# Attention with grouped keys: values cast to DRAM by batch and filled over SyncE, GpSimd transfers placed in planned gaps

## The chip, the cores and the metric

The kernel runs on one core of a Trainium2 chip. The metric is the device time of one execution in microseconds (us). It is measured in several runs, of which the median is taken. One more execution is recorded by the hardware profiler, and all rows of instructions below come from it.

## The reference

Grouped-query attention: 8 batches, 8 query heads, 2 heads of keys and values (each serves 4 query heads), 1024 positions, head size 64, all in float32.

```
scores = scale * np.matmul(q_group, k_group.transpose(0, 1, 3, 2))
scores_max = np.max(scores, axis=-1, keepdims=True)
attn = np.exp(scores - scores_max)
attn = attn / (np.sum(attn, axis=-1, keepdims=True) + 1e-08)
output[:, q_start:q_end, :, :] = np.matmul(attn, v_group)
```

The inputs are small (0.1 times a normal draw), and the kernel takes the exponential without subtracting the maximum.

## The kernel before, in words

**Tiling.** One query head of one batch is a job; there are 64 jobs. A job has 8 chunks of 128 keys. For a chunk, two matmuls (L856) write the scores of 128 keys against 1024 queries into one of three PSUM slots `sp`: keys lie on the partitions. The exponential of 372 of the 512 chunks is taken by ScalarE (L866, tile `pt`). That of the other 140 is made by VectorE from bits: a pass over PSUM writes 16-bit integers `yt` (L877); two operations on bits take from them a mantissa `zt` (L884) and a power of two `et` (L891), for two chunks at a time (2048 columns); and a multiplication `zt = yt * zt` (L900) corrects the mantissa. Part of the columns of this multiplication is given to GpSimd (L829), 107 times in all. These are called products below. TensorE then multiplies 128 x 128 blocks of `pt`, `et` and `zt` with the values `va`, which carry a column of ones, so that the sums of the softmax come along (L918). VectorE takes the reciprocal (L983), scales into `ost` (L992), and SyncE stores (L996).

**Order.** A class `Plan` lays out the work of ScalarE, VectorE and TensorE ahead of time with fixed costs (the `M_` constants, in ns) and gives a list of events with due times. The kernel emits instructions in the order of these times, and each engine runs its own list in that order. The order of scores, exponentials, passes and products is therefore fixed when the kernel is built. A product on GpSimd is made to wait for the instruction of VectorE that stands before it, so that it starts as VectorE begins a pass over PSUM.

**Transfers.** Queries and keys are first cast from float32 to bfloat16 by a transfer that GpSimd issues from DRAM to DRAM (`cast_q`, `cast_k`, both through `cast`, L617; the tiles `qd`, `kd`). One transfer of queries takes two heads, one of keys takes both heads of a batch. SyncE then brings them into SBUF transposed: `turn_q` (L677) and `turn_k` (L667), whose result is doubled with the two halves exchanged by `copy_k` (L671, L672). Values are cast straight into SBUF: for each of the 15 groups (a batch and one of its two heads of keys and values) after the first, `cast_v` (L659) issues two transfers from GpSimd into one of four buffers `va`. The values of the first group come another way and are not touched.

The due times of these transfers hang on `at`, the planned time of a job's first score: 19 us ahead for keys, 18 for queries, 12 for values. Once the first product has been emitted, a cast that becomes due is put into a list and begun behind a product if the planned gap to the next product is longer than `M_ISSUE`, 650 ns:

```
nth += 1
while casts and starts[nth] > free + M_ISSUE:
    begin(*casts.pop(0)[1:], False)
    free += M_ISSUE
```

A cast that is over 5 us overdue is begun at once. Each engine's instructions run in order, so a product behind a cast on GpSimd waits for the cast's issue, and on SyncE a copy of `kt` or a store waits for all that stand before it.

Of the kernel before, what the change touches and what calls it, by code (L numbers as in the profile page):

```python
# [10 lines left out]
M_START = 5450  # L11
# [25 lines left out]
M_GLEAD = 160  # L37
M_GFIX = 190
M_GCOL = 1.88
# [2 lines left out]
M_NORM = 531  # L42
M_HOLD = 1500
M_SPARE = 800
M_ISSUE = 650

M_GAP = 90
M_RUNWAY = 2100
# [9 lines left out]
INF = float("inf")  # L58
# [479 lines left out]
def kernel(  # L538
# [7 lines left out]
    nc = tc.nc  # L546
    FP32 = mybir.dt.float32
    BF16 = mybir.dt.bfloat16
# [5 lines left out]
    B, H, S, D = q.shape  # L554
    G = k.shape[1]
# [3 lines left out]
    HS = S // 2  # L559
# [10 lines left out]
    NVA = 4  # L570
    plan = Plan(NJ, NPT - 2, NCT - 1, NYT - 2)

    dram = ctx.enter_context(tc.tile_pool(name="dram", bufs=1, space=bass.MemoryType.DRAM))
# [34 lines left out]
    va = [kvp.tile([128, NH, 2, D + 1], BF16, name=f"va{i}") for i in range(NVA)]  # L608
# [2 lines left out]
    nc.vector.memset(warm, 0.0)  # L611
    for t in va:
        nc.vector.memset(t[:, :, :, D : D + 1], 1.0)
    kt, qt, qd, kd, vs = {}, {}, {}, {}, {}

    def cast(src, t):
        return nc.gpsimd.dma_start(  # L617
            out=t.rearrange("(a x) d -> a (x d)", a=128),
            in_=src.rearrange("(a x) d -> a (x d)", a=128),
        )  # L620

    def cast_q(j):
        b, h = divmod(j, H)
        if j == NJ - 1:
            t = qd[j] = dram.tile([HS, 2 * D], BF16, name=f"qd{j}")
            return nc.gpsimd.dma_start(  # L626
                out=t.rearrange("(c p) d -> p c d", p=128), in_=rows(q[b, h], True)
            )
        n = 2 if 3 < j < NJ - 2 else 1
        t = dram.tile([n * HS, 2 * D], BF16, name=f"qd{j}")  # L630
        for i in range(n):
            qd[j + i] = t[i * HS : (i + 1) * HS, :]
        return cast(q.rearrange("b h s d -> (b h s) d")[j * S : (j + n) * S, :], t)
# [9 lines left out]
    def rows(x, fours=False):  # L643
        how = "(p c two) d -> p c (two d)" if fours else "(c p two) d -> p c (two d)"
        return x.rearrange(how, p=128, two=2)
# [9 lines left out]
            in_=vs.pop((b, g)).rearrange("p c (two d) -> p c two d", two=2),  # L655
        )

    def cast_v(b, g, two):
        return nc.gpsimd.dma_start(  # L659
            out=va[(b * G + g) % NVA][:, :, two, 0:D],  # L660
            in_=v[b, g].rearrange("(c p two) d -> p c two d", p=128, two=2)[:, :, two, :],
        )

    def turn_k(b, g):
        t = ktp.tile([128, 2, HS], BF16, name="kt")
        kt[(b, g)] = t
        nc.sync.dma_start_transpose(out=t[:, 0:1, :], in_=kd[(b, g)])  # L667

    def copy_k(b, g):
        t = kt[(b, g)]  # L670
        nc.sync.dma_start(out=t[D : 2 * D, 1, :], in_=t[0:D, 0, :])  # L671
        nc.sync.dma_start(out=t[0:D, 1, :], in_=t[D : 2 * D, 0, :])  # L672
# [69 lines left out]
    for c in range(NH):  # L742
        for half in range(2):
            lo = half * D
# [12 lines left out]
    ev = list(plan.ev)  # L757
    n = len(ev)
    for j in range(NJ):
        b, h = divmod(j, H)  # L760
        at = need[j]
        g = h // HPG
        if h % HPG == 0 and j:
            if g == 0 or b == 0:
                ev.append((max(at - 19000, M_START + 200), "ck", None, (b, g), None))
            ev.append((at - 12500, "tk", None, (b, g), None))
            ev.append((at - 4000, "cp", None, (b, g), None))
            for two in range(2):
                ev.append((at - 12000, "cv", None, (b, g, two), None))
        if j == 0:  # L770
            ev.append((M_START + 100, "pl", None, (b, g), None))
        if j == 3 or (j > 3 and j % 2 == 0) or j == NJ - 1:
            ev.append((max(at - 18000, M_START + 100), "cq", None, j, None))
        if j > 1:
            ev.append((max(at - 11000, M_START + 100 * j), "tq", None, j, None))
    for x in [e for e in plan.ev if e[1] == "norm"]:
        lo, hi = x[2]
# [13 lines left out]
    def flat(t):  # L791
        return t.bitcast(BF16).rearrange("p i a b -> p (i a b)")
# [11 lines left out]
                yield ci, pt[(j, c)][:, par, :]  # L804

    begun = [e for e in ev if e[1] == "gmul"]
    starts = [e[0] + M_GLEAD for e in begun] + [INF]
    nth, free = 0, 0
    casts = []
    vec, gps = None, None  # L810

    def begin(kind, j, gate):
        ins = cast_q(j) if kind == "cq" else (cast_k if kind == "ck" else cast_v)(*j)
        if now and gate:
            tc.add_manual_dep(ins.ins, now.ins.name, Sync, reason="loads in time, not sooner")

    for when, kind, x, j, c, *cols in ev:
        if casts and casts[0][0] < when - 5000:
            begin(*casts.pop(0)[1:], True)
        if kind in ("ck", "cq", "cv"):  # L820

            if gps is None:
                begin(kind, j, True)
            else:
                casts.append((when, kind, j))
        elif kind == "gmul":
            lo, w = c
            z = flat(zt[j])[:, lo : lo + w]
            gps = nc.gpsimd.tensor_tensor(  # L829
                out=z, in0=flat(yt[j])[:, lo : lo + w], in1=z, op=ALU.mult  # L830
            )
            tc.add_manual_dep(gps.ins, vec.ins.name, Sync, reason="VectorE needs the port before")

            took = M_GFIX + M_GCOL * w
            free = max(free, when + M_GLEAD) + took
            nth += 1
            while casts and starts[nth] > free + M_ISSUE:
                begin(*casts.pop(0)[1:], False)
                free += M_ISSUE
        elif kind == "tk":  # L840
            turn_k(*j)
        elif kind == "cp":
            copy_k(*j)
        elif kind == "tq":
# [3 lines left out]
        elif kind == "score":  # L848
            b, h = divmod(j, H)
            t = kt[(b, h // HPG)]  # L850
            where_s[(j, c)] = new_slot(x)

            for half in range(2):
                lo = half * D
# [8 lines left out]
        elif kind == "act":  # L863
            p = pp.tile([128, 2, HS], BF16, name="pt")
# [7 lines left out]
        elif kind == "dpass":  # L872
            ch, i = j
            where[c] = j
            if i == 0:
                yt[ch] = yp.tile([128, CHN, 2, HS], U16, name="yt")
            vec = nc.vector.tensor_scalar(  # L877
                out=yt[ch][:, i, :, :], in0=where_s[c],
                scalar1=EXP_A, scalar2=EXP_B, op0=ALU.mult, op1=ALU.add,
            )  # L880
        elif kind == "zh":
# [3 lines left out]
                out=zt[j][:, 0:c], in0=yt[j][:, 0:c], scalar1=0x7F, scalar2=0x3F00,  # L885
                op0=ALU.bitwise_and, op1=ALU.bitwise_or,
            )
        elif kind == "two":
# [3 lines left out]
                out=et[j][:, 0:c], in0=yt[j][:, 0:c], scalar1=0x7F80, scalar2=None,  # L892
# [5 lines left out]
        elif kind == "mul":  # L898
            z = flat(zt[j])[:, 0 : cols[0]]
            vec = nc.vector.tensor_tensor(  # L900
                out=z, in0=flat(yt[j])[:, 0 : cols[0]], in1=z, op=ALU.mult
            )
        elif kind == "add":
            z = zt[j].bitcast(BF16)[:, 0:c]
            vec = nc.vector.tensor_tensor(
                out=z, in0=et[j].bitcast(BF16)[:, 0:c], in1=z, op=ALU.add
            )
        elif kind == "pv":
            job, piece = divmod(x, NPIECE)
            b, h = divmod(job, H)  # L910
            qs, par = divmod(piece, 2)
            lo = (x - plan.groups[plan.group_of[x]][0]) * (D + 1)
# [3 lines left out]
            for i in range(j, j + c):  # L916
                ci, p = every[i]
# [9 lines left out]
        elif kind == "pvf":  # L927
# [4 lines left out]
            for i in range(NPIECE):  # L932
# [3 lines left out]
                lo = i % 4 * (D + 1)  # L936
# [9 lines left out]
        elif kind == "pvl":  # L946
            b, h = divmod(NJ - 1, H)
# [3 lines left out]
            for i in range(NPIECE):  # L951
# [4 lines left out]
                lo = i % 4 * (D + 1)  # L956
# [9 lines left out]
        elif kind in ("rec", "norm"):  # L966
            lo, hi = x
            n = hi - lo
# [24 lines left out]
        elif kind == "store":  # L993
            b, h = divmod(j, H)
            r = place_of(j * NPIECE)
            ins = nc.sync.dma_start(  # L996
                out=rows(out[b, h], j in (0, NJ - 1)),
                in_=ost[:, r : r + NPIECE, :].rearrange("p (s two) d -> p s (two d)", two=2),
# [32 lines left out]
```

## Time and profile before

| what | value |
|---|---|
| time, median of 3 runs | 360.22 us (359.57 to 360.33) |
| the profiled execution, its own time | 360.52 us |
| its span, first to last instruction | 358.7 us |
| granted clock of TensorE | 1.00 |
| mean busy share of the DMA engines from 100 to 200 us | 0.76 |
| GpSimd: casts of values, of queries and keys | 30 of 858 ns, 41 of about 615 ns |
| GpSimd: products | 107 of 1240 ns |

Rows of the profile name the line of the kernel, the engine (PE is TensorE, PEld its weight loads, DVE VectorE, ACT ScalarE, POOL GpSimd, SP SyncE), the operation, what is written and read, and how often. After the bar stand the busy time in us and the mean length of one in ns; after the second bar the idle time of the engine ahead of such instructions, and what ended it. In a timeline the first number is the start in us, the second the length in us of what is merged in the row, and the bracket gives idle time before it. In a list of waits a row has who waited, for whom, the sum in us, the number and the longest. A q after an engine's name means its instruction queue.

### The profile page before, as it was taken

How to read it: one execution, taken by the hardware profiler on the slowest of the kernel's cores; microseconds unless marked ns; L12 is line 12 of the kernel's file. 1: busy time of each engine (PE TensorE's matmuls, PEld its weight loads, DVE VectorE, ACT ScalarE, POOL GpSimd, SP SyncE). 2: the span in 40 equal slices, each digit the busy share in tenths (PEclk: the TensorE clock that was granted, in tenths of full speed). 3: DMA queues.
4: the chain of work that ended last, by engine and by line, in shares of the span. 5: the costliest groups of instructions: out<-in, count | busy, mean ns of one | idle time of the engine just before them, and what ended most of it. 6: DMA issues, size and time to landing. Idle time of an engine off the chain costs nothing.

```text
span 358.7 us, 14051 instructions
## 1 busy us (share of the span) xinstructions
PE 346.6 (97%) x6236; PEld 222.4 (62%) x6236; DVE 348.4 (97%) x516; ACT 346.3 (97%) x376; POOL 182.9 (51%) x186
## 2 busy tenths in 40 slices
PE   8899999999999999999999999999999999999994
PEld 3556666666666666666566666566666666666664
DVE  4999999999999999999999999999999999999994
ACT  5999999999999999999999999999999999999991
POOL 4227656575375645566485755455655626670000
PEclk9999999999999999999999999999999999999999
DMA  6955959279686954888567786837969687594233
GB/s 146 134 103 106 162 116 134 50 127 142 133 135 119 149 134 76 129 137 123 121 87 136 148 134 112 134 103 114 107 135 120 133 151 103 120 114 109 37 101 106
DMA packets 96173, 42.87 MB, mean 119 GB/s; under 512 B 61024, under 2 KB 94944, under 8 KB 95456
## 3 DMA queue, kind: packets, MB, share of 16 engines
q1 hardware_dynamic: 78288, 29.51, 39.0%
q0 software_dynamic: 17680, 12.19, 31.3%
q8 instruction: 49, 0.80, 1.0%
q10 hardware_dynamic: 144, 0.26, 0.3%
q14 instruction: 12, 0.10, 0.1%
HBM read 25.17 MB, written 27.00 MB: 145 GB/s over the span
## 4 chain that ended last, share of the span: by engine, by line
ACT 37%; DVE 34%; PE 24%; issue 3%; DMA 1%; SPq 0%
ACT pt L866 37%; DVE yt L877 18%; PE ops L918 12%; PE sp L856 10%; DVE zt L900 4%; DVE et L891 4%; DVE ost L992 4%; DVE zt L884 3%; DMA kt<-kt 1%; PE ops L710 1%; DVE rec L983 1%; PE sp L958 1%; PE sp L733 0%; PE ops L745 0%; SPq L671 0%
## 5 line engine op out<-in xcount | busy, mean ns | idle before, releaser
L866 ACT ACTIVATE pt<-sp 128x1024 bf16<-128x1024 f32 x372 | 343.8, 1036 | 1.9 <-PE sp L856 1.5
L829 POOL TENSOR_TENSOR zt<-yt,zt 128x448 bf16<-128x448 bf16 (+2 forms) x107 | 132.7, 1240 | 132.4 <-DVE et L891 48.6
L856 PE MATMUL sp<-qt,kt 64*128 64x512 bf16 x1024 | 172.7, 383 | 5.6 <-DVE yt L877 3.4
L918 PE MATMUL ops<-va,pt 128*128 128x65 bf16 x2872 | 175.4, 194 | 0.0
L877 DVE TENSOR_SCALAR yt<-sp 128x1024 uint16<-128x1024 f32 x140 | 169.3, 1209 | 0.8 <-PE sp L856 0.8
L918 PEld LDWEIGHTS <-pt 128*128 128x128 bf16 x2872 | 127.8, 97 | 34.2 <-issue 34.2
L918 PE MATMUL ops<-va,zt 128*128 128x65 bf16 x1096 | 127.6, 194 | 0.0
L918 PE MATMUL ops<-va,et 128*128 128x65 bf16 x1048 | 117.9, 194 | 0.0
L918 PEld LDWEIGHTS <-zt 128*128 128x128 bf16 x1096 | 87.4, 97 | 14.6 <-issue 14.0
L918 PEld LDWEIGHTS <-et 128*128 128x128 bf16 x1048 | 82.3, 98 | 17.7 <-issue 17.7
L856 PEld LDWEIGHTS <-kt 64*128 64x128 bf16 x1024 | 47.8, 93 | 58.0 <-issue 36.4
L900 DVE TENSOR_TENSOR zt<-yt,zt 128x896 bf16<-128x896 bf16 (+9 forms) x71 | 55.0, 775 | 0.0
L884 DVE TENSOR_SCALAR zt<-yt 128x2048 uint16<-128x2048 uint16 (+1 forms) x71 | 48.6, 685 | 0.2
L891 DVE TENSOR_SCALAR et<-yt 128x2048 uint16<-128x2048 uint16 (+1 forms) x71 | 47.7, 677 | 0.0
L992 DVE TENSOR_TENSOR ost<-ops,rec 128x448 f32<-128x448 f32 (+2 forms) x73 | 44.1, 604 | 0.1
L659 POOL DMA_DIRECT2D va<-in_v_dram x30 | 25.7, 858 | 3.1 <-PE sp L856 2.4
L617 POOL DMA_DIRECT2D qd<-in_q_dram x33 | 20.2, 612 | 1.2 <-POOLq L1015 0.8
L983 DVE RECIPROCAL rec<-ops 128x7 f32<-128x7 f32 (+2 forms) x73 | 14.0, 191 | 0.0
L710 PE MATMUL ops<-warm 128*128 128x128 bf16 (+1 forms) x36 | 5.7, 296 | 1.7 <-DVE warm L611 1.2
L710 PEld LDWEIGHTS <-warm 128*128 128x128 bf16 x36 | 2.8, 108 | 4.9 <-issue 3.7
L617 POOL DMA_DIRECT2D kd<-in_k_dram x8 | 5.0, 625 | 0.0
L626 POOL DMA_DIRECT2D qd<-in_q_dram x1 | 0.8, 759 | 8.0 <-PE sp L856 8.0
(38 smaller groups left out, 28.6 us busy)
## 6 DMA issues: line engine op xcount, KB each, us to landing
out_dram<-ost SPq DMA_DIRECT2D x64, 256.0 KB, 3.2
qd<-in_q_dram POOLq DMA_DIRECT2D x29, 256.0 KB, 5.1
va<-in_v_dram POOLq DMA_DIRECT2D x30, 64.0 KB, 4.3
kt<-kt SPq DMA_DIRECT2D x30, 64.0 KB, 4.2
kd<-in_k_dram POOLq DMA_DIRECT2D x7, 256.0 KB, 4.2
qt<-qd SPq DMA_TRANSPOSE x63, 3.5
qd<-in_q_dram POOLq DMA_DIRECT2D x5, 128.0 KB, 4.1
q<-in_q_dram ACTq DMA_DIRECT2D x1, 256.0 KB, 3.1
```

Of the source, the lines that this page charges most:

```text
L617: return nc.gpsimd.dma_start(out=t.rearrange("(a x) d -> a (x d)", a=128), in_=src.rearrange("(a x) d -> a (x d)", a=128),)
L659: return nc.gpsimd.dma_start(out=va[(b * G + g) % NVA][:, :, two, 0:D], in_=v[b, g].rearrange("(c p two) d -> p c two d", p=128, two=2)[:, ...
L829: gps = nc.gpsimd.tensor_tensor(out=z, in0=flat(yt[j])[:, lo : lo + w], in1=z, op=ALU.mult)
L856: now = nc.tensor.matmul(sps[x][:, half, :], lhsT=t[lo : lo + D, c // NH, ci % NH * 128 : (ci % NH + 1) * 128], rhs=qt[j][lo : lo + D, 0, ...
L866: exps.append(nc.scalar.activation(out=p, in_=where_s[(j, c)], func=AF.Exp, scale=scale))
L877: vec = nc.vector.tensor_scalar(out=yt[ch][:, i, :, :], in0=where_s[c], scalar1=EXP_A, scalar2=EXP_B, op0=ALU.mult, op1=ALU.add,)
L884: vec = nc.vector.tensor_scalar(out=zt[j][:, 0:c], in0=yt[j][:, 0:c], scalar1=0x7F, scalar2=0x3F00, op0=ALU.bitwise_and, op1=ALU.bitwise_or,)
L891: vec = ins = nc.vector.tensor_scalar(out=et[j][:, 0:c], in0=yt[j][:, 0:c], scalar1=0x7F80, scalar2=None, op0=ALU.bitwise_and,)
L900: vec = nc.vector.tensor_tensor(out=z, in0=flat(yt[j])[:, 0 : cols[0]], in1=z, op=ALU.mult)
L918: nc.tensor.matmul(ops[plan.group_of[x] % 2][:, lo : lo + D + 1], lhsT=p[:, qs * 128 : (qs + 1) * 128], rhs=va[(b * G + h // HPG) % NVA][: ...
L983: vec = nc.vector.reciprocal(out=to, in_=sums)
L992: vec = nc.vector.tensor_tensor(out=to, in0=o, in1=by, op=ALU.mult)
```

## The change

Three things are changed.

- Values are cast as keys are: one transfer of GpSimd for both heads of a batch, from DRAM to DRAM (`cast_v`, tile `vd`). The new `fill_v` brings a group's values from there into `va`, by two transfers that SyncE issues. It is due 5 us ahead of the group's first score, 1 us ahead of the copies of `kt`.
- The casts are due earlier: keys 25 us ahead, values 22, queries 24.
- The gap for each cast is chosen before the emission. For every product the planned end is worked out, and the room up to the next one. A cast that is due after the first product takes the first gap within `M_LATE` (8.5 us) of its due time that has `M_ISSUE` (now 900 ns) of room left, or the one with the most room if there is none. It is emitted behind that product. The list of waiting casts, and the rule for overdue ones, go.

The order of instructions on TensorE, VectorE and ScalarE stays as it is, and so does that of the products. GpSimd issues 22 casts fewer; SyncE issues 30 transfers more.

```
--- before.py
+++ after.py
@@ -42,7 +42,8 @@
 M_NORM = 531
 M_HOLD = 1500
 M_SPARE = 800
-M_ISSUE = 650
+M_ISSUE = 900
+M_LATE = 8500
 
 M_GAP = 90
 M_RUNWAY = 2100
@@ -611,7 +612,7 @@
     nc.vector.memset(warm, 0.0)
     for t in va:
         nc.vector.memset(t[:, :, :, D : D + 1], 1.0)
-    kt, qt, qd, kd, vs = {}, {}, {}, {}, {}
+    kt, qt, qd, kd, vd, vs = {}, {}, {}, {}, {}, {}
 
     def cast(src, t):
         return nc.gpsimd.dma_start(
@@ -655,11 +656,20 @@
             in_=vs.pop((b, g)).rearrange("p c (two d) -> p c two d", two=2),
         )
 
-    def cast_v(b, g, two):
-        return nc.gpsimd.dma_start(
-            out=va[(b * G + g) % NVA][:, :, two, 0:D],
-            in_=v[b, g].rearrange("(c p two) d -> p c two d", p=128, two=2)[:, :, two, :],
-        )
+    def cast_v(b, g):
+        n = G - g
+        t = dram.tile([n * HS, 2 * D], BF16, name=f"vd{b}_{g}")
+        for i in range(n):
+            vd[(b, g + i)] = t[i * HS : (i + 1) * HS, :]
+        lo = (b * G + g) * S
+        return cast(v.rearrange("b g s d -> (b g s) d")[lo : lo + n * S, :], t)
+
+    def fill_v(b, g):
+        src = vd[(b, g)].rearrange("(c p) (two d) -> p c two d", p=128, two=2)
+        for two in range(2):
+            nc.sync.dma_start(
+                out=va[(b * G + g) % NVA][:, :, two, 0:D], in_=src[:, :, two, :]
+            )
 
     def turn_k(b, g):
         t = ktp.tile([128, 2, HS], BF16, name="kt")
@@ -762,15 +772,15 @@
         g = h // HPG
         if h % HPG == 0 and j:
             if g == 0 or b == 0:
-                ev.append((max(at - 19000, M_START + 200), "ck", None, (b, g), None))
+                ev.append((max(at - 25000, M_START + 200), "ck", None, (b, g), None))
+                ev.append((max(at - 22000, M_START + 300), "cv", None, (b, g), None))
             ev.append((at - 12500, "tk", None, (b, g), None))
             ev.append((at - 4000, "cp", None, (b, g), None))
-            for two in range(2):
-                ev.append((at - 12000, "cv", None, (b, g, two), None))
+            ev.append((at - 5000, "fv", None, (b, g), None))
         if j == 0:
             ev.append((M_START + 100, "pl", None, (b, g), None))
         if j == 3 or (j > 3 and j % 2 == 0) or j == NJ - 1:
-            ev.append((max(at - 18000, M_START + 100), "cq", None, j, None))
+            ev.append((max(at - 24000, M_START + 100), "cq", None, j, None))
         if j > 1:
             ev.append((max(at - 11000, M_START + 100 * j), "tq", None, j, None))
     for x in [e for e in plan.ev if e[1] == "norm"]:
@@ -804,9 +814,21 @@
                 yield ci, pt[(j, c)][:, par, :]
 
     begun = [e for e in ev if e[1] == "gmul"]
-    starts = [e[0] + M_GLEAD for e in begun] + [INF]
-    nth, free = 0, 0
-    casts = []
+    ends, room, then = [], [], {}
+    for e in begun:
+        at = max(e[0] + M_GLEAD, ends[-1] if ends else 0)
+        ends.append(at + M_GFIX + M_GCOL * e[4][1])
+    for e, end in zip(begun[1:], ends):
+        room.append(e[0] + M_GLEAD - end)
+    room.append(INF)
+    for e in ev:
+        if e[1] in ("ck", "cq", "cv") and e[0] > begun[0][0]:
+            fit = [i for i, x in enumerate(ends) if e[0] <= x < e[0] + M_LATE]
+            fits = [i for i in fit if room[i] >= M_ISSUE]
+            i = fits[0] if fits else max(fit, key=lambda i: room[i])
+            room[i] -= M_ISSUE
+            then.setdefault(i, []).append(e)
+    nth = 0
     vec, gps = None, None
 
     def begin(kind, j, gate):
@@ -815,14 +837,10 @@
             tc.add_manual_dep(ins.ins, now.ins.name, Sync, reason="loads in time, not sooner")
 
     for when, kind, x, j, c, *cols in ev:
-        if casts and casts[0][0] < when - 5000:
-            begin(*casts.pop(0)[1:], True)
         if kind in ("ck", "cq", "cv"):
 
             if gps is None:
                 begin(kind, j, True)
-            else:
-                casts.append((when, kind, j))
         elif kind == "gmul":
             lo, w = c
             z = flat(zt[j])[:, lo : lo + w]
@@ -831,14 +849,13 @@
             )
             tc.add_manual_dep(gps.ins, vec.ins.name, Sync, reason="VectorE needs the port before")
 
-            took = M_GFIX + M_GCOL * w
-            free = max(free, when + M_GLEAD) + took
+            for _, what, _, who, _ in then.get(nth, []):
+                begin(what, who, False)
             nth += 1
-            while casts and starts[nth] > free + M_ISSUE:
-                begin(*casts.pop(0)[1:], False)
-                free += M_ISSUE
         elif kind == "tk":
             turn_k(*j)
+        elif kind == "fv":
+            fill_v(*j)
         elif kind == "cp":
             copy_k(*j)
         elif kind == "tq":
```

## The prediction

> **What bounds the kernel now.** I read the page from its first part to its costliest groups, then the timelines of single engines, then the queue of SyncE. The page:
>
> ```profile
> span 358.7 us, 14051 instructions
> ...
> PE 346.6 (97%) x6236; PEld 222.4 (62%) x6236; DVE 348.4 (97%) x516; ACT 346.3 (97%) x376; POOL 182.9 (51%) x186
> ...
> ACT 37%; DVE 34%; PE 24%; issue 3%; DMA 1%; SPq 0%
> ...
> L866 ACT ACTIVATE pt<-sp 128x1024 bf16<-128x1024 f32 x372 | 343.8, 1036 | 1.9 <-PE sp L856 1.5
> L829 POOL TENSOR_TENSOR zt<-yt,zt 128x448 bf16<-128x448 bf16 (+2 forms) x107 | 132.7, 1240 | 132.4 <-DVE et L891 48.6
> ...
> L659 POOL DMA_DIRECT2D va<-in_v_dram x30 | 25.7, 858 | 3.1 <-PE sp L856 2.4
> L617 POOL DMA_DIRECT2D qd<-in_q_dram x33 | 20.2, 612 | 1.2 <-POOLq L1015 0.8
> ```
>
> Three engines are 97% busy and share the chain. No transfer time can be won here directly; a gain must come out of the chain of ScalarE, VectorE and TensorE. ScalarE's idle time (1.9 us) understates it, because one pass lasts 1.03 us while the next starts about 0.92 us after it: a start that is late by under 0.11 us shows no gap. The timeline of ScalarE, merged where no gap shows:
>
> ```profile
> 6.47 141.79 ACT L866 ACTIVATE pt<-sp 128x1024 bf16<-128x1024 f32 x153 [0.62 <-PE sp L856]
> 148.43 23.07 ACT L866 ACTIVATE pt<-sp 128x1024 bf16<-128x1024 f32 x25 [0.17 <-PE sp L856]
> 171.74 1.02 ACT L866 ACTIVATE pt<-sp 128x1024 bf16<-128x1024 f32 x1 [0.24 <-PE sp L856]
> 173.00 61.43 ACT L866 ACTIVATE pt<-sp 128x1024 bf16<-128x1024 f32 x66 [0.24 <-PE sp L856]
> 234.67 116.87 ACT L866 ACTIVATE pt<-sp 128x1024 bf16<-128x1024 f32 x127 [0.24 <-PE sp L856]
> ```
>
> The last piece is the calm one: (116.87 - 1.03) / 126 = 0.919 us a step. All 371 steps (6.47 to the last start at 350.5) took 344.0 us; at 0.919 they would take 340.9. So **3.1 us** is the most that better timing can give ScalarE. Where it goes is seen at the worst place, 171 us. First GpSimd, then VectorE:
>
> ```profile
> 166.23 1.67 POOL L659 DMA_DIRECT2D va<-in_v_dram  x2
> 167.91 1.44 POOL L829 TENSOR_TENSOR zt<-yt,zt 128x448 bf16<-128x448 bf16 x1
> 169.31 0.69 POOL L617 DMA_DIRECT2D qd<-in_q_dram  x1
> 170.01 1.04 POOL L829 TENSOR_TENSOR zt<-yt,zt 128x448 bf16<-128x448 bf16 x1
> ```
>
> ```profile
> 167.89 0.58 DVE L900 TENSOR_TENSOR zt<-yt,zt 128x832 bf16<-128x832 bf16 x1
> 168.39 1.52 DVE L884 TENSOR_SCALAR zt<-yt 128x2048 uint16<-128x2048 uint16 x1
> 169.83 1.21 DVE L877 TENSOR_SCALAR yt<-sp 128x1024 uint16<-128x1024 f32 x1
> ```
>
> Two value casts hold GpSimd for 1.67 us. The product behind them is meant to run beside the pass over PSUM that starts at 166.76, and starts at 167.91 instead. It is still running when VectorE comes to L884, which then takes 1.52 us (median 0.68) and ends when the product ends. The next pass frees its PSUM slot late, TensorE scores late (it waits 0.66 us for L877 at 171.1), and ScalarE starts 0.34 us late twice.
>
> **What the Trainium skill says.** "SBUF — State Buffer", § SBUF: two separate sides: VectorE and GpSimd share a pair of ports under an exclusive lock; whichever instruction starts first, a VectorE instruction in a two-port mode or with two SBUF inputs or a GpSimd one, keeps the pair to its end, and the other waits. The trace agrees: 1.52 against 0.68. The same section says that a DMA issued from GpSimd cannot write its descriptors while VectorE holds the pair, and that one issued from SyncE is untouched. The trace agrees on the first: the key cast at 71.26 takes 0.74 us beside an L884 and ends just after it; such casts take a median 0.565. "DMA: Bandwidth & Descriptors", § SWDGE vs HWDGE vs iDMA: a cast must be issued from GpSimd. So the cast stays there; only the placing can move.
>
> **The change, part by part.**
>
> *Removed from GpSimd:* 30 value casts, 25.7 us. *Added:* 8 casts of values to DRAM (one for batch 0, one for each of seven batches), shaped like a key or query cast: 8 x 0.565 = 4.5 us. GpSimd is idle half its time, so the 21 us themselves are worth nothing; their places are worth something.
>
> *Moved:* every cast behind the first product. In the timeline of GpSimd before, a cast stands in 47 gaps between products, and in 24 of them the next product starts within 0.04 us of the cast's end: it was pushed. For the changed program I took the product behind which each cast stands and read that gap in the trace of before, casts taken out: 40 casts in 38 gaps. 36 gaps are at least 1.21 us long (two casts go into gaps of 2.0 and 3.1 us). Only two are short: 0.66 us behind product 64 and 0.94 behind product 81. A cast of 0.57, or 0.78 at worst, fits into 37.
>
> *What that gives:* going through VectorE's L884, L891 and L900, 16 beside or behind casts are longer than their kind by 0.08 to 0.84 us, together 3.6 us. ScalarE's late starts (step minus 0.92) that follow these within a few us: 0.15 at 42.6, 0.09 at 57.4, 0.30 at 82.7 to 84.5, 0.27 at 148.4, 0.68 at 171.7 and 173.0, 0.09 at 193, 0.37 at 212.9 and 214.9, 0.49 at 232 to 234.7: **2.4 us**, two thirds of the 3.6. The rest of the 3.1 has no cast beside it (0.3 at 22 to 24, 0.15 at 116.8, smaller ones); I leave it. Bounds: 3.1 if casts cost those too, 1.2 if half the stretching comes back in the new places.
>
> *New collisions:* product 64 starts about 0.1 us late, and a cast can still meet a two-port instruction that starts just after it (the query cast at 255.10 lengthened one by 0.04). I take **0.2 us**; 0 to 0.8.
>
> *Added to SyncE:* 30 fills of `va` (64 KB, 512 runs). The nearest row is the store, also 512 runs: 0.38 us to issue, 1.89 at most. 30 x 0.38 = 11 us on a queue that mostly waits:
>
> ```profile
> SPq L996 <- DVE ost L992: 84.6, 41, 6.5
> SPq L677 <- DMA qd<-in_q_dram: 57.4, 23, 5.7
> ```
>
> The second row should shrink, since casts become due 6 us earlier. A fill waits for its cast (due 22 us ahead of the head, issued at latest 13.5 ahead, landing in 5) and stands 5 us ahead. Behind it in order are the two copies of `kt`, transposes and stores. The copies' spare time between landing and first use (scores' order laid on ScalarE's starts, an estimate) is 4.2 us in the twelfth group, 5.2 in the thirteenth, 6 to 10 elsewhere. Two fills cost 0.8 to 1.2, against a due time 1.0 earlier: covered, **0**; at the worst price see rival C. The values are first multiplied some 15 us after the fill's landing (4.3): covered.
>
> *DMA engines:* 15,360 packets of 128 B took 43 ns each from GpSimd's queue. The new casts have packets like the query casts (16 of 1.78 us a cast, about 0.2 ms of engine time for all), and the fills run at about 23 to 30 ns, the price of 256 and 512 B packets of SyncE's queue. Sum 0.56 to 0.67 ms against 0.66: no more load. **0**, from -0.1 to +0.3.
>
> *Start:* early casts (a query pair at about 8.5 us, keys and queries of batch 1 before the first product) come earlier, while two casts of 512 small packets leave. The transposes of heads 3 and 4 land 2.9 and 2.6 us ahead of use: covered, **0**.
>
> **Sum** against the profiled execution (360.52; span 358.7 and 1.8 around it): 360.52 - 2.4 + 0.2 = 358.3. It stands 0.3 above the median, 360.22, so I forecast **358.0**.
>
> **The rivals.** *A, the gaps are not what the plan says.* Casts move to other products and push those. For: about half the casts before pushed a product. Against: 37 of 38 measured gaps are long enough. Half of 2.4 left: 360.2 - 1.2 + 0.2 = 359.2. *B, VectorE's time comes free but not ScalarE's,* as each of the three engines is 97% busy and another releases last: 360.2 give or take 0.3. Against: at 171 us the wait names L877, so the link is seen. *C, slower: the fills hold SyncE's queue.* Place: the copies of `kt` behind them. A copy's issue took up to 3.0 us (L671)[...], and copies then land behind 1,024 packets, 64 on each engine at 43 ns, 2.8 us. At 2.2 us a fill: 4.4 - 1.0 + 2.8 = 6.2 us late, stalls of 2.0, 1.0 and 0.3 in the three tightest groups, 3.4 less the gain of 2.2: 361.4. It decides from about 2.1 us a fill; at 3.0 each it costs 12 us. Against: the median issue of 512 runs is 0.38.
>
> **Numbers.** Forecast 0.68 (own range 357.2 to 359.0), A 0.12, B 0.08, C 0.12. A measurement tells 0.2%, 0.72 us, from no change: 359.50 to 360.94. Faster takes the forecast and most of A, 0.78; same takes B and the rest of A, 0.10; slower is C, 0.12. The range goes from 356.9 (all 3.1 and a little) to 360.2, and leaves out C and half of B.
>
> **What would show it.** Right: L884's maximum falls below 0.9 us, products no longer start at a cast's end, ScalarE's pieces join into steps of 0.92, its last start comes near 348.2, and SyncE's wait for `qd` shrinks. Wrong: idle time of TensorE at L856 released by a DMA of `kt` (C), L884 still near 1.5 (A), or VectorE's busy time down by 3 us and the span not (B).

## The result, and the profile after

The changed kernel took **357.33 us** (median of 10 runs, 356.07 to 358.53), the kernel before, measured beside it, 359.80 (10 runs, 358.83 to 360.49). The ratio is 0.9932, with a 95% interval of 0.9912 to 0.9951: faster by 2.5 us. Measured twice more, beside the experiments below, it gave 0.9936 and 0.9922. The recorded execution took 358.14 us and so stands 0.8 above its median; a likely reason is seen at the start of the run, and it matters for every row read from it.

The page after:

```profile
span 356.4 us, 14072 instructions
...
PE 346.9 (97%) x6236; PEld 223.9 (63%) x6236; DVE 345.5 (97%) x516; ACT 344.8 (97%) x376; POOL 159.6 (45%) x164
...
ACT 70%; PE 23%; DMA 4%; issue 1%; DVE 1%; SPq 0%; POOL 0%
```

GpSimd lost 23 us of work, and VectorE 2.9. VectorE, 34% of the chain of waits before, is 1% of it now. ScalarE has 70%, and what holds the end now is ScalarE's own rate.

The timelines of GpSimd and then of VectorE at the place that the prediction took as the worst, 166 to 171 us. What was L884 is now L901:

```profile
166.56 1.03 POOL L847 TENSOR_TENSOR zt<-yt,zt 128x448 bf16<-128x448 bf16 x1 [0.63 <-DVE et L908]
168.86 1.03 POOL L847 TENSOR_TENSOR zt<-yt,zt 128x448 bf16<-128x448 bf16 x1 [1.27 <-DVE zt L901]
```

```profile
167.53 0.57 DVE L917 TENSOR_TENSOR zt<-yt,zt 128x832 bf16<-128x832 bf16 x1
168.03 0.68 DVE L901 TENSOR_SCALAR zt<-yt 128x2048 uint16<-128x2048 uint16 x1
168.63 1.21 DVE L894 TENSOR_SCALAR yt<-sp 128x1024 uint16<-128x1024 f32 x1
```

The product starts at 166.56, with the pass over PSUM that it is meant to run beside, and is done before L901 comes. L901 takes 0.68 us, where L884 took 1.52. Over the whole run its spread (minimum, median, maximum in ns) says the same; the line of before stands first:

```profile
L884 DVE TENSOR_SCALAR zt<-yt x71: 369/679/1518, 9.9 to 349.4; 128x2048 uint16<-128x2048 uint16 x69, 128x1024 uint16<-128x1024 uint16 x2
L901 DVE TENSOR_SCALAR zt<-yt x71: 375/682/719, 9.3 to 347.3; 128x2048 uint16<-128x2048 uint16 x69, 128x1024 uint16<-128x1024 uint16 x2
```

None of VectorE's two-port operations (L901, L908, L917) is stretched by over 0.055 us; 16 were before, by 3.7 us together. ScalarE's timeline is in one piece for 355 passes, but it is not whole:

```profile
6.07 11.11 ACT L883 ACTIVATE pt<-sp 128x1024 bf16<-128x1024 f32 x12 [0.41 <-PE sp L873]
17.70 4.79 ACT L883 ACTIVATE pt<-sp 128x1024 bf16<-128x1024 f32 x5 [0.52 <-PE sp L873]
23.25 326.35 ACT L883 ACTIVATE pt<-sp 128x1024 bf16<-128x1024 f32 x355 [0.76 <-PE sp L873]
```

Two late starts, at 17.70 and 23.25, are new. The chain of waits, in order of time, leads back from the first:

```profile
6.49 0.55 POOL va L654
7.04 3.27 DMA qd<-in_q_dram
10.31 0.02 issue
10.33 6.68 DMA qt<-qd
17.01 0.05 issue
17.06 0.41 PE sp L873 x2
```

The transpose of head 3's queries takes 6.68 us to land. In the trace before, the same one went from 10.14 to 13.43, 3.29 us. SyncE's timeline of before, and the landing of this one transfer:

```profile
10.14 1.13 SPq L677 DMA_TRANSPOSE qt<-qd  x1
...
DMA to landing us min/median/max: 3.3/3.3/3.3
```

Ahead of it two casts have now been issued that came later before (the values at 10.57, the queries at 12.86). GpSimd's timeline, first of before and then of after:

```profile
7.69 0.49 POOL L617 DMA_DIRECT2D kd<-in_k_dram  x1
10.57 2.02 POOL L659 DMA_DIRECT2D va<-in_v_dram  x2 [2.40 <-PE sp L856]
```

```profile
8.00 0.49 POOL L618 DMA_DIRECT2D kd<-in_k_dram  x1
8.47 0.49 POOL L618 DMA_DIRECT2D vd<-in_v_dram  x1
8.95 0.49 POOL L618 DMA_DIRECT2D qd<-in_q_dram  x1
```

TensorE waits 1.25 us for that transpose, and a second loss follows. The windows of 1 us show it; the columns are the stretch, its length, the busy times (and instructions) of PE, PEld, DVE, ACT and POOL, TensorE's granted clock, the DMA share and GB/s:

```profile
18.00:19.00 1.00, 0.49 (x6) 0.11 (x3) 1.00 (x2) 1.00 (x2) 0.45 (x1) 1.00 0.58 131
19.00:20.00 1.00, 1.00 (x11) 0.69 (x8) 1.00 (x2) 1.00 (x2) 0.33 (x1) 0.62 1.68 246
20.00:21.00 1.00, 1.00 (x9) 0.42 (x6) 1.00 (x2) 1.00 (x2) 0.16 (x1) 0.50 0.08 17
21.00:22.00 1.00, 1.00 (x14) 0.65 (x13) 1.00 (x2) 1.00 (x2) 0.86 (x1) 0.50 2.24 292
22.00:23.00 1.00, 1.00 (x20) 0.87 (x19) 0.86 (x2) 0.49 (x1) 0.23 (x2) 0.67 0.91 101
```

From about 19.3 to 22.7 us TensorE is busy throughout with 9 to 14 matmuls a us, at half its clock, and ScalarE's next scores are late again. The Trainium skill, "TensorE: Matmul & The Clock Gate", § Part 1: The HAM clock gate (the "warmup" mystery), says that the clock is halved after an idle window of about 3.4 us, and that the windows run free of the program. The length agrees: 3.4 us at 0.50. No idle of that length stands ahead of it here, though; the longest is the 1.25 us. In the 3.41 us ahead of the fall at 19.24 TensorE was busy for 1.67 us, half the time.

So the recorded difference of the spans, 358.7 to 356.4, has parts that partly cancel. The table compares the two recorded executions; step times are from ScalarE's start of one pass to that of another.

| part | before | after | difference |
|---|---|---|---|
| first pass of ScalarE starts at | 6.47 | 6.07 | -0.40 |
| first 25 steps | 23.12 | 24.42 | +1.30 |
| the other 346 steps | 320.89 (927.4 ns each) | 318.00 (919.1 ns) | **-2.89** |
| last start to the end of the span | 8.26 | 7.87 | -0.39 |

The first row moves from one recorded execution to another of one kernel (5.73 and 6.08 in e1 below), and no weight is put on it.

### The profile page after: what moved, and what is told of

Read it like the earlier page. It is cut to its first block, busy times and chain, and to the rows that moved or that the text cites. A ratio compares the mean times of both kernels' runs of the same rounds, so it can differ in the third digit from the quotient of the medians.

```text
span 356.4 us, 14072 instructions
## 1 busy us (share of the span) xinstructions
PE 346.9 (97%) x6236; PEld 223.9 (63%) x6236; DVE 345.5 (97%) x516; ACT 344.8 (97%) x376; POOL 159.6 (45%) x164
## 3 DMA queue, kind: packets, MB, share of 16 engines
q1 hardware_dynamic: 94128, 31.48, 44.5%
q0 software_dynamic: 2096, 12.19, 24.6%
## 4 chain that ended last, share of the span: by engine, by line
ACT 70%; PE 23%; DMA 4%; issue 1%; DVE 1%; SPq 0%; POOL 0%
ACT pt L883 70%; PE ops L935 12%; PE sp L873 10%; DMA qt<-qd 2%; DMA vs<-in_v_dram 1%; DMA qd<-in_q_dram 1%; PE sp L975 1%; PE ops L720 0%; DVE yt L894 0%; SPq L704 0%; DVE ost L1009 0%; POOL va L654 0%; DVE rec L1000 0%
## 5 line engine op out<-in xcount | busy, mean ns | idle before, releaser
L917 DVE TENSOR_TENSOR zt<-yt,zt 128x896 bf16<-128x896 bf16 (+9 forms) x71 | 53.7, 756 | 0.0
L901 DVE TENSOR_SCALAR zt<-yt 128x2048 uint16<-128x2048 uint16 (+1 forms) x71 | 47.5, 669 | 0.2
L908 DVE TENSOR_SCALAR et<-yt 128x2048 uint16<-128x2048 uint16 (+1 forms) x71 | 46.8, 663 | 0.0
L618 POOL DMA_DIRECT2D qd<-in_q_dram x33 | 18.9, 572 | 2.0 <-PE sp L873 1.2
L618 POOL DMA_DIRECT2D vd<-in_v_dram x8 | 4.5, 561 | 0.0
L922 DVE TENSOR_TENSOR zt<-et,zt 128x2048 bf16<-128x2048 bf16 (+1 forms) x4 | 4.3, 1072 | 0.0
```

The costliest lines, as they stand in the source:

```text
L618: return nc.gpsimd.dma_start(out=t.rearrange("(a x) d -> a (x d)", a=128), in_=src.rearrange("(a x) d -> a (x d)", a=128),)
L901: vec = nc.vector.tensor_scalar(out=zt[j][:, 0:c], in0=yt[j][:, 0:c], scalar1=0x7F, scalar2=0x3F00, op0=ALU.bitwise_and, op1=ALU.bitwise_or,)
L908: vec = ins = nc.vector.tensor_scalar(out=et[j][:, 0:c], in0=yt[j][:, 0:c], scalar1=0x7F80, scalar2=None, op0=ALU.bitwise_and,)
L917: vec = nc.vector.tensor_tensor(out=z, in0=flat(yt[j])[:, 0 : cols[0]], in1=z, op=ALU.mult)
```

## The experiments

Theory **T**, the prediction's: GpSimd's value casts stretched VectorE's operations; without them ScalarE loses no time there. Three questions were open. Which half does it, the values by way of DRAM or the planned gaps? What of a value cast does the harm: a pushed product, its destination or its length? What do the early casts at the start cost? Unless said otherwise a kernel differs from the changed one by the diff shown. Kernels measured together share the runs of the kernel before, whose medians were 360.22 for the first four, 359.47 for the next four and 359.89 for the last three.

| kernel | median us (range) | ratio to before | 346 steps, us | stretched, sum us | pushed |
|---|---|---|---|---|---|
| e1, both early casts held | 356.72 (356.14–357.16) | 0.9908 [0.9891, 0.9924] | 317.91 | 0 | 1 |
| e2, values by DRAM only | 357.17 (356.51–358.47) | 0.9922 [0.9902, 0.9943] | 318.52 | 3, 0.92 | 12 |
| e3, planned gaps only | 358.38 (357.28–359.67) | 0.9957 [0.9941, 0.9973] | 319.20 | 10, 1.83 | 2 |
| e4, shortest gaps | 357.18 (356.98–358.17) | 0.9926 [0.9910, 0.9942] | 318.12 | 1, 0.26 | 25 |
| changed again | 357.02 (356.57–358.33) | 0.9936 [0.9917, 0.9955] | 317.98 | 0 | 1 |
| e5, queries held | 356.84 (356.18–357.43) | 0.9924 [0.9907, 0.9941] | 317.93 | 0 | 1 |
| e6, values held | 356.76 (356.34–357.24) | 0.9920 [0.9903, 0.9937] | 317.93 | 0 | 1 |
| e8, long issues to DRAM | 357.67 (356.96–357.88) | 0.9946 [0.9930, 0.9961] | 318.34 | 4, 0.76 | 1 |
| changed, third time | 356.82 (356.28–357.06) | 0.9922 [0.9908, 0.9936] | 317.91 | 0 | 1 |
| e1 again | 356.67 (356.06–356.91) | 0.9915 [0.9900, 0.9930] | 317.99 | 0 | 1 |
| e7, fills twice | 359.97 (357.57–361.73) | 1.0000 [0.9983, 1.0017] | 318.89 | 0 | 1 |

"346 steps" is as in the table above; the kernel before has 320.89, with 16 stretched operations and 24 pushed products. A product counts as pushed if it starts within 0.04 us of a cast's end. An operation counts as stretched if it is over 0.06 us longer than others of its shape. Two of e7's 22 runs, 363.92 and 365.70 us, stand far from the rest and are left out of its row.

**Which half does it.** e2 is the kernel before with the values by way of DRAM; the rule of 650 ns, the list of waiting casts and the due times of keys and queries stay:

```
-            for two in range(2):
-                ev.append((at - 12000, "cv", None, (b, g, two), None))
+            ev.append((at - 5000, "fv", None, (b, g), None))
...
+                ev.append((max(at - 18500, M_START + 300), "cv", None, (b, g), None))
```

> The kernel before with the first part of the change alone: values cast by batch to DRAM and filled over SyncE; due times of keys and queries, the 650 ns rule and the list of waiting casts stay. Theory 1 (the gain is products no longer pushed by casts into VectorE's two-port instructions, and the pairs of value casts of 0.83 to 1.0 us each made the large pushes): few stretched instructions are left, 357.3 to 358.2. Rival (the gain comes from casts being earlier, so that SyncE no longer waits for query casts): 359.8, as before, with SyncE's wait for qd still above 40 us.

e3 is the changed kernel with the values cast straight into SBUF by 30 transfers, each in a planned gap:

```
-            ev.append((at - 5000, "fv", None, (b, g), None))
+            for two in range(2):
+                ev.append((max(at - 19000, M_START + 300), "cv", None, (b, g, two), None))
```

> The changed kernel with the values cast straight into SBUF as before (30 transfers of GpSimd, due 19 us ahead), each placed in a planned gap of 900 ns or more. Theory 1 (the place decides, not the number of casts on GpSimd): no VectorE instruction stretched by over 0.1 us beyond its kind after 30 us, save one at product 64; 357 to 358, the head as in the changed kernel or a little worse. Rival (fewer transfers on GpSimd is what helps): 359 or more.

e2 took 3.05 us off, as much as the whole change within the intervals. SyncE's wait for `qd` is still 46.6 us in it, so earlier casts are not what brings the gain. e3 took 1.84 off, and stretched operations are left in it although it has two pushed products where 24 were before. The timelines of e3's GpSimd and VectorE show how:

```profile
174.98 1.79 POOL L660 DMA_DIRECT2D va<-in_v_dram  x2
177.35 1.03 POOL L838 TENSOR_TENSOR zt<-yt,zt 128x448 bf16<-128x448 bf16 x1 [0.58 <-DVE et L897]
```

```profile
174.98 0.69 DVE L890 TENSOR_SCALAR zt<-yt 128x2048 uint16<-128x2048 uint16 x1
175.58 1.68 DVE L897 TENSOR_SCALAR et<-yt 128x2048 uint16<-128x2048 uint16 x2
177.18 1.21 DVE L883 TENSOR_SCALAR yt<-sp 128x1024 uint16<-128x1024 f32 x1
```

The gap is long enough, and no product is late. But two L897 take 1.68 us together, where the median of one is 0.68, while two value casts are being issued. So a cast alone can hold VectorE, and a planned gap doesn't help against that. By this reading, 7 of e3's 10 stretched operations (1.1 us) stand beside a value cast with no product in between, as did 5 of the 16 before (0.9 of 3.7 us). Each half alone thus brings most of the gain, and the two do not add up. e3 also begins its casts earlier, which wasn't separated.

**Does a pushed product matter?** e4 is the changed kernel with each cast in the gap with the *least* room, one cast to a gap:

```
-            i = fits[0] if fits else max(fit, key=lambda i: room[i])
-            room[i] -= M_ISSUE
+            i = min(fit, key=lambda i: room[i])
+            room[i] += 1e6
```

> The changed kernel, but each cast goes into the shortest gap within 8.5 us of its due time, one cast a gap; the trace of the changed kernel gives such gaps 0.63 to 0.66 us, against a cast of 0.55, or up to 0.85 beside L901 and L908. Theory 1: products are pushed by up to 0.2 us again, some VectorE instructions are stretched, 358.0 to 359.0. Rival (earliness and number of casts decide): 357.3 as the changed kernel.

25 products are pushed, one more than before the change, and one operation is stretched; the time is that of the changed kernel, not the 358 to 359 expected. GpSimd's and VectorE's timelines of e4 show why nearly all of these products do no harm:

```profile
69.31 1.51 POOL L847 TENSOR_TENSOR zt<-yt,zt 128x704 bf16<-128x704 bf16 x1 [0.88 <-PE ops L935]
70.78 0.71 POOL L618 DMA_DIRECT2D vd<-in_v_dram  x1
71.51 1.04 POOL L847 TENSOR_TENSOR zt<-yt,zt 128x448 bf16<-128x448 bf16 x1
```

```profile
71.30 1.23 DVE L894 TENSOR_SCALAR yt<-sp 128x1024 uint16<-128x1024 f32 x1
72.43 0.63 DVE L917 TENSOR_TENSOR zt<-yt,zt 128x896 bf16<-128x896 bf16 x1
```

The product starts 0.2 us after the pass beside which it is meant to run. It lasts 1.04 us, the pass 1.23, so it ends (72.55) just 0.12 us into the next two-port operation, which takes 0.63 us where one of the same shape at 67.94 takes 0.58. 24 of the 25 products start so, 0.19 to 0.22 us after their pass. That is not late: the 83 products of the kernel before that are not pushed start 0.08 to 0.27 us after theirs. The count of pushed products takes in many that are on time. The 25th, at 119.10, is late: it starts 0.55 us after its pass, and the multiplication at 119.70 takes 0.89 us where all other traces have 0.63.

The kernel before divides in the same way. Its 13 products behind casts of queries or keys started 0.16 to 0.20 us after their pass, on time, and stretched nothing. Its 11 products behind value casts, which last longer and mostly come in pairs, started 0.39 to 1.15 us after theirs, and each stretched an operation: 2.9 of the 3.7 us. Every one of these operations is longer by the time that the product still had to run when it began, less 0.12 us, to within 0.01; it is as if it waited for the product and then ran in whole. What counts is how late a product starts, not that a cast stands right ahead of it.

**Destination or length?** e8 is e1 (below) with the values cast to DRAM group by group, in rows laid out so that each of the 15 transfers has 512 runs, as each of the old ones had; each stands in a planned gap:

```
+        t = vd[(b, g)] = dram.tile([HS, 2 * D], BF16, name=f"vd{b}_{g}")
+        return nc.gpsimd.dma_start(
+            out=t.rearrange("(c p) d -> p c d", p=128), in_=rows(v[b, g])
+        )
```

> The kernel with the start held back (356.7), with the values cast to DRAM one head at a time in 512 short runs a transfer (15 of them), each in a planned gap of 900 ns. Only the shape of the transfer is the old one; target, number per gap and fills over SyncE are the new ones. Theory 1 (a transfer of 512 runs takes GpSimd 0.76 to 1.0 us to issue, long enough to reach into the next two-port instruction of VectorE, where one of 16 runs takes 0.55): a third of the 15, some 3 to 6, stretch an instruction by 0.1 to 0.2 us; 356.9 to 357.6. Rival (writing into SBUF is what made the value casts harmful): no instruction stretched, 356.7.

The issue takes 0.80 us instead of 0.56, though it writes to DRAM, and stretching is back. The spread of the new casts, then GpSimd, then VectorE at 218 us:

```profile
L661 POOL DMA_DIRECT2D vd<-in_v_dram x15: 759/802/931, 12.8 to 304.7; - x15
```

```profile
216.53 1.64 POOL L845 TENSOR_TENSOR zt<-yt,zt 128x768 bf16<-128x768 bf16 x1 [0.82 <-DVE rec L998]
218.12 0.91 POOL L661 DMA_DIRECT2D vd<-in_v_dram  x1
```

```profile
215.67 0.68 DVE L906 TENSOR_SCALAR et<-yt 128x2048 uint16<-128x2048 uint16 x1
...
218.64 0.88 DVE L906 TENSOR_SCALAR et<-yt 128x2048 uint16<-128x2048 uint16 x1
```

The product has ended (218.17) before L906 begins at 218.64. L906 takes 0.20 us longer than the one at 215.67, beside the cast alone. The same is seen at 47.62, by 0.10. At 195.97 a multiplication is 0.20 longer beside the product that a cast of 0.93 us has pushed to 0.41 us after its pass; in e5, with a short cast there, it starts 0.21 after it. The fourth stretched operation, at 87.79, is not a cast's: a product stands beside it that had waited for TensorE, with no cast ahead. So 3 of the 15 casts stretch an operation.

A target in SBUF isn't needed for the stretching. How much of the gain hangs on the shape of the casts, e8 shows less well. It is 0.8 to 0.9 us slower than e5 and e6, measured with it, and five of its six runs are slower than all twelve of theirs, but its interval overlaps with those of both and of the changed kernel. In the recorded executions its 346 steps lose 0.4 us against theirs, of which 0.2 come behind the operation at 87.79. e8 differs from e1 in the number of casts as well (15 for 8), and that part wasn't separated.

The length on record is not what tells the casts apart. In e4 the casts of 16 packets took a median of 0.71 us and up to 0.91, which was not followed up, and stretched nothing by themselves. Over the 13 recorded executions 109 two-port operations begin 0.25 to 0.6 us ahead of the end of such a cast with no product beside them, and none is longer by over 0.04 us. Of the 15 that begin so ahead of the end of a cast of 512 runs, 14 are longer, by 0.09 to 0.28.

**The start.** Three kernels hold back one or both casts that stand ahead of head 3's transpose. e1 holds both:

```
-                ev.append((max(at - 22000, M_START + 300), "cv", None, (b, g), None))
+                ev.append((max(at - 22000, M_START + 7000), "cv", None, (b, g), None))
...
-            ev.append((max(at - 24000, M_START + 100), "cq", None, j, None))
+            ev.append((max(at - 24000, M_START + (7000 if j > 4 else 100)), "cq", None, j, None))
```

> The changed kernel, with two things of the start held back: the value cast of batch 0 and the query cast of heads 6 and 7 are due 7 us after the plan's start instead of 0.3 and about 3 us. Theory 1 (the stall at 17 to 25 us, where TensorE waits for the transposed queries of head 3, comes from these two casts standing ahead of that transpose on the DMA engines): the transpose lands in about 3.3 us instead of 6.7, the two late starts of ScalarE (1.68 and 1.78 us a step) go, the time falls to 355.6 to 356.2. Theory 2 (the stall is chance, or comes from the granted clock that drops to 0.67 there): 357.3, as the changed kernel.

e5 has the second of these edits alone, e6 the first alone; beside them the changed kernel was run again.

> The changed kernel once more, on the same chip as the next runs, as the measure for them: 357.3 give or take 0.6 by the earlier runs. It should again show a transpose of head 3 that lands 5 us or more after its issue, and a late start of ScalarE at about 17 us.

> The changed kernel with only the query cast of heads 6 and 7 held back to 7 us after the plan's start; the value cast of batch 0 stays at 8.5 us. Theory (each cast of the start puts 16 KB or 8 KB packets of up to 1.8 us each ahead of the transpose on all 16 DMA engines; the query cast is the larger, 512 KB read against 256 KB): most of the stall goes, the transpose of head 3 lands in about 4.3 us, 356.5. If both count alike: 357.0. If the stall is chance: as the changed kernel.

> The changed kernel with only the value cast of batch 0 held back; the query cast of heads 6 and 7 stays early. Theory (the query cast is the larger load): the transpose of head 3 still lands 5 to 6 us after its issue, the stall stays in greater part, 357.0 to 357.4. If the value cast alone is the cause: 356.6 with no stall.

In e1 ScalarE's timeline joins into one piece:

```profile
5.73 341.95 ACT L883 ACTIVATE pt<-sp 128x1024 bf16<-128x1024 f32 x372 [0.26 <-PE sp L873]
```

From first to last start these are 340.9 us, 0.919 a step, which is just what the prediction worked out as the least. The transpose of head 3 landed after 4.4 us in e1, 5.0 in e5 and 5.9 in e6, and the first 25 steps took 22.93 us in e1 and 23.13 in both others, as in the kernel before. Taking one of the two casts away is enough. For e6, in which the stall was expected to stay, that is a surprise. The medians hardly show it: e1 stays above the 355.6 to 356.2 expected, and e5 and e6 are 0.18 and 0.26 us below the changed kernel, with intervals that overlap. So both ends were measured once more together:

> The changed kernel, on the same chip and in the same rounds as the two runs below, to tell whether holding back the start is worth something beyond the noise: a ratio to the kernel before of 0.993.

> The changed kernel with both casts of the start held back, beside it on one chip. If the stall at 17 us costs what the two traces show (ScalarE's delay at 30 us is 1.4 to 1.5 us with it, -0.4 to 0.6 without), the ratio is 0.990 and the time 0.7 to 1.3 us under the changed kernel; if the trace shows an exceptional execution, 0.993.

0.15 us, not the 0.7 to 1.3 that the traces had let expect, and again the intervals overlap. The recorded executions say why it is so little: the stall isn't the same each time. In the one of the third measurement TensorE waited 1.11 us at the same place and kept its full clock, and the first 25 steps took 23.45 us; in the first two its clock fell, and they took 24.42 and 24.52. In e4, which has the early casts too, it waited the same 1.25 us, kept its clock, and the steps took 23.59. So some 0.5 us are the wait's, and 1.0 the clock's. The place of the wait may decide. In both executions whose clock fell, it fell 13.65 us, four times 3.41, after it had risen at the start, and in the 3.41 us ahead of the fall TensorE was busy for 0.49 and 0.46 of the time. Stretches of 3.41 us, counted in the same way from the rise of the clock, have 0.58 in e4 and 0.62 in the third measurement where the wait begins, since they hold more work ahead of it. Four executions fit this and don't prove it. Of the 22 runs of the changed kernel 8 are above 357.2 us, of the 11 of e1 none; this speaks for a stall whose price varies, but those runs carry no profile, so it isn't shown. In a recorded execution holding the casts was worth 0.5 to 1.6 us; in the medians it is 0.15 to 0.26, which these runs cannot tell from nothing.

**Rival C, pushed on purpose.** e7 is e1 with each fill issued twice:

```
-        for two in range(2):
+        for two in (0, 1, 0, 1):
```

> The kernel with the start held back, with each fill of the values issued twice (60 transfers on SyncE instead of 30), the second pair behind the landing of the first, since it writes the same place. If SyncE's queue has room to spare, as the wait for stores of over 100 us says, then no more than 0.3 us is lost; if the fills' place ahead of the copies of kt is what is near its limit (spare time 2.6 us at the least in the changed kernel's trace, and a landing takes 3.3), TensorE waits for kt in one or two groups, 357.0 to 359.

3.3 us slower than e1 beside it, above the 357 to 359 expected: the whole gain is gone. The second pair writes what the first does and has to wait for it, so this is more than twice the issues. SyncE's waits in e7 say so, and TensorE's timeline shows where it comes through:

```profile
SPq L670 <- DMA va<-vd: 36.1, 29, 2.7
```

```profile
202.39 0.61 PE L873 MATMUL sp<-qt,kt 64*128 64x512 bf16 x4 [0.96 <-DMA qt<-qd]
```

```profile
203.04 1.02 ACT L883 ACTIVATE pt<-sp 128x1024 bf16<-128x1024 f32 x1 [0.51 <-PE sp L873]
```

A loss of rival C's kind occurs here, 0.9 us in two late starts of ScalarE, but its victim is the transpose of queries, not the copies of `kt` that the prediction named. The recorded execution of e7 (357.77 us) is one of its fastest; a worse one was not recorded, so where its slower runs lose the rest is open.

No version here is clearly better than the changed kernel. e1 has the lowest ratios, by less than the measurement can tell.

## Why the prediction was right, and where it was not

**The time.** 358.0 was forecast, 357.33 measured, in the likeliest case's own range. The sum for the recorded execution was 358.3 against 358.14; that it is so close is partly luck, as the table of parts shows.

- **The gain, 2.4: right in kind, somewhat small.** Late starts beside casts went away, VectorE's chain share fell to 1%, and 346 steps gave 2.89 us. The prediction left out 0.7 of the possible 3.1, since no cast stood beside it. About 0.5 of that came with the rest, and in e1, whose steps have no stall at the start, all of it; on what it hung was not followed up.
- **New collisions, 0.2: none.** No stretched operation is left in the changed kernel's traces. One product is pushed, as forecast for product 64.
- **Removed, "worth nothing": failed.** The prediction put taking away 30 value casts at nothing and gave the whole 2.4 to the new places. e2 has the old rule for places and the full gain; e3 has the value casts in new places and 1.84 of it.
- **The link from a cast to VectorE: right for most of it.** Products made late by value casts did 2.9 of the 3.7 us of stretching. But "24 of 47 gaps hold a pushed product" counts 13 that started on time beside 11 that were late. And L884 at 168.39 does not end "when the product ends": the product ends at 169.35 and L884 at 169.91, so it ran nearly in whole behind it. The other 0.9 us, from value casts with no product in between, the prediction had among its 16 operations but gave no cause of their own. For casts it took from the Trainium skill, "SBUF — State Buffer", § SBUF: two separate sides, that VectorE can hold up the writing of their descriptors. e3 and e8 show the other direction, a cast of 512 runs that holds up VectorE, by 0.09 to 0.28 us.
- **Start, "covered, 0": failed.** The transposes of heads 3 and 4 were given 2.9 and 2.6 us of spare time and no load. Head 3's took 3.4 us longer behind two more casts, and the first 25 steps lost 1.3 us in the recorded execution. In the medians side by side the loss is 0.15 to 0.26.
- **Fills on SyncE, 0: right, with less to spare.** A fill took 0.53 us to issue, not 0.38, and 1.43 at most, under the 2.1 from which rival C decides:

```profile
L670 SPq DMA_DIRECT2D va<-vd x30: 361/526/1430, 18.2 to 315.4; - x30
```

By the same estimate as in the prediction the copies of `kt` had 2.6 us to spare in the two tightest groups, where it gave 4.2 for the tightest before. SyncE's waits moved as said: that for `qd`, 57.4 us before, nearly went, and the one for stores took up the time:

```profile
SPq L1013 <- DVE ost L1009: 111.5, 46, 6.8
...
SPq L687 <- DMA qd<-in_q_dram: 7.3, 3, 3.8
```

- **DMA load, 0: right, from a price too high.** The fills' packets of 128 B took 14 ns each, where 23 to 30 was assumed, against 43 from GpSimd's queue. The share of GpSimd's queue fell from 31.3 to 24.6%, that of the SyncE queue rose from 39.0 to 44.5.
- **The rivals.** A (casts push other products) did not occur; in e4 even the shortest gaps made just one product late, so with casts of 16 packets it would have cost little. B is refuted: VectorE's time became ScalarE's almost one to one, 2.9 us each. C did not decide; e7 shows a loss of its kind, by way of the queries.

## What to carry to other kernels

On GpSimd, ask how many runs a DMA has before asking where to put it. Here casts of 16 large packets, put into the shortest gaps, made one of 25 products late; casts of 512 runs made 11 late by 0.4 us and more, and reached into VectorE's two-port operations from planned gaps too. And where a product must not meet VectorE's next operation, measure how late it starts, not whether a cast stands ahead of it. When casts are made early, count what stands ahead of the first transposes, where everything still waits on transfers. And compare the recorded executions part by part: a sum that fits can hold a gain of 2.9 and a loss of 1.3.

## What the runs showed of the hardware

- A two-port operation of VectorE that began while a product of GpSimd ran was longer by the rest of the product less 0.12 us, to within 0.01 (11 cases before the change).
- One that began 0.28 to 0.44 us ahead of the end of a cast of 512 runs was longer by 0.09 to 0.28 us in 14 of 15 cases (before, e3, e8); beside casts of 16 packets none was, in 109.
- A wait of 1.25 to 1.33 us in a thinly used stretch was followed by some 3.4 us of half clock on TensorE in two recorded executions (the changed kernel, first and second), and one of 1.25 us was not in another (e4), nor one of 1.11 (the changed kernel, third).
- 512 runs cost GpSimd 0.80 us to issue (median in e8), and 16 packets of 16 KB, of twice the bytes, 0.55 (median in the changed kernel; 0.71 in e4).
- A transpose with two more casts ahead of it landed after 5.7 to 7.5 us (the changed kernel three times, e4); with neither of them ahead, after 2.9 to 4.4 (before, e1 twice, e7, e8).
